# A fused decoder layer on one core: two more pairs by seven products in the down projection, and the low parts of 14 tiles made by an accumulating DMA

## The chip, the core and the metric

The kernel runs on one core of a Trainium2 chip. The metric is the device time of one execution in microseconds (us), the median of several runs: 1047.4 us for the kernel before (three runs, 1047.33 to 1047.88).

## The reference

One layer with 256 tokens and width 2048: two kinds of attention side by side, an output projection, and an MLP. Only the MLP's second product matters here, `u @ w_down`, where `u` is 256 x 8192 and `w_down` 8192 x 2048, all float32:

```python
x = x + _rmsnorm(mixed @ w_out[layer], norm_attn_post[layer])

h = _rmsnorm(x, norm_mlp_pre[layer])
u = jnp.square(jax.nn.relu(h @ w_up[layer]))
x = x + _rmsnorm(u @ w_down[layer], norm_mlp_post[layer])
```

## The kernel before, in words

**Three passes for one float32 product.** TensorE multiplies in the rounded type fp32r. So each operand is split into a high part `hi` (the value rounded, written by ScalarE, ACT, L306) and a low part `lo` (the value less its high part, a subtraction on VectorE, DVE, L307). A product is `hi*hi + hi*lo + lo*hi`, three matmuls of 128x128 by 128x512 (`three`, L1016).

**The down projection** (from L1197) has two halves `c`, each 1024 columns of `w_down`. In a half the 64 row blocks of 128 rows, `k`, go by in order; two of them make a pair `kp`. There are two ways through a pair:

- *ordinary* (`"k"`): each of the two row blocks is a tile of 128x1024 (512 KB), loaded by SP into one of five buffers `raw`, split by ACT and DVE into `hi` and `lo` (eight buffers each), and used by 4 products: 8 products, 24 matmuls in the pair.
- *by seven products* (`"w"`): the pair is treated as a 2x2 block matrix by a Strassen-like scheme (`seven_products`, L1021): 7 products, 21 matmuls, but from four tiles (`b11`, `b`, `u`, `t`). The pair's 1,024 KB come by one DMA on GpSimd's queue (POOL, L374) into the buffers `ab_down` and `c` in turn (`load_two`, `seven_down`). DVE forms sums of them (`sums`, L361, L365, L366) into `st_down`, and the four tiles are split as ordinary tiles are. The left operand needs sums too: three small DVE instructions (`four_sums`, L977 to L979, into `st_down`) and a split into `s`.

`DOWN_SEVEN` (L117) lists the pairs by seven products: 7, 11, 13, 17, 19, 23, 25 and 29 in the first half, the odd ones from 3 to 27 in the second. `SHARED` lists those in both; their `s` is written to DRAM in the first half (`keep_s`) and read back in the second (`down_back`, POOL). In the first half the low parts `ulo` of `u`, one group for every two pairs, are made on DVE and written to DRAM (`keep_u`); the second half reads them back on POOL (L960).

**What sets the order.** Everything is written out at build time; each engine and each DMA queue works through its own list in order, and semaphores hold an instruction until its operands and its buffer are ready. `Weights.emit` (L193) writes a tile's load and split seven tiles ahead of its products. `plan_seven` (L406) hangs a seven-product pair's `fetch` and `sums` in front of the tile that is two tiles before the pair's first (`SUMS_AHEAD`), though not before the end of the preceding seven-product pair. Where seven-product and ordinary pairs alternate, `fetch` and `sums` of a pair therefore stand right behind the four tiles of the seven-product pair before it, and in front of the ordinary pair in between. `Weights.emit` is where ordinary tiles are split.

Of the kernel before, what the change touches and what calls it, by code (L numbers as in the profile page):

```python
# [18 lines left out]
F32 = mybir.dt.float32  # L19
# [3 lines left out]
AF = mybir.ActivationFunctionType  # L23
OP = mybir.AluOpType
# [77 lines left out]
def up_steps(first, *groups):  # L102
    steps = [("k", k) for k in first]
    for i, ks in enumerate(groups):
# [9 lines left out]
N_SEVEN = [sum(w == "w" for w, _ in steps) for steps in UP_STEPS]  # L114


DOWN_SEVEN = ((7, 11, 13, 17, 19, 23, 25, 29), range(3, 28, 2))  # L117
SHARED = [k for k in DOWN_SEVEN[0] if k in DOWN_SEVEN[1]]
GT = FF // 512
DOWN_STEPS = [[s for kp in range(2 * GT)  # L120
               for s in ([("w", kp)] if kp in ws else [("k", 2 * kp), ("k", 2 * kp + 1)])] for ws in DOWN_SEVEN]

# [5 lines left out]
class Flow:  # L128
# [3 lines left out]
    def __init__(self):  # L132
        self.clock = 0.0
        self.chains = []
# [34 lines left out]
class Weights:  # L169


    def __init__(self, nc, pool, split, bufs, ahead):
        self.nc, self.pool, self.split_fn = nc, pool, split
        self.bufs, self.limit, self.ahead = bufs, bufs, ahead
        self.specs, self.tiles, self.done = [], [], []
        self.first, self.after = {}, {}

    def plan(self, *spec):


        self.specs.append(spec)
        self.done.append(False)
        return len(self.specs) - 1
# [9 lines left out]
    def emit(self, upto):  # L193
        upto = min(upto, self.done.index(False) + self.limit, len(self.specs))
        while len(self.tiles) < upto:
            i = len(self.tiles)
            spec = self.specs[i]
            make = len(spec) == 1
            for f in self.first.pop(i, ()):
                f()  # L200
            if not make:
                src, nk, n, g = (*spec, None)[:4]
                w = nk * n
                raw = self.load(src if len(src.shape) == 3 else src.rearrange("(k p) n -> p k n", p=P), w, f"raw{i}")
                for f in self.after.pop(i, ()):
                    f()
            hi = self.pool.tile([P, CW], F32R, tag="hi", bufs=self.bufs, name=f"hi{i}")
            lo = self.pool.tile([P, CW], F32R, tag="lo", bufs=self.bufs, name=f"lo{i}")
            if make:
                spec[0](hi, lo)  # L210
                self.tiles.append((hi, lo))
                continue

            def v(t):
                return t[:, :w].rearrange("p (k n) -> p k n", k=nk)

            cuts = [(o, min(o + 512, w)) for o in range(0, w, 512)] if i < FINE else [(0, w)]
            for o, e in cuts:
                self.split_fn(hi[:, o:e], lo[:, o:e], raw[:, o:e], g)
            self.tiles.append((v(hi), v(lo)))  # L220
# [43 lines left out]
def layer(nc, tc, io):  # L264
# [52 lines left out]
    weights = Weights(nc, wp, split, W_BUFS, W_AHEAD)  # L317
# [23 lines left out]
    def up_weight(j, k):  # L341
        return io["w_up"][k * P:(k + 1) * P, j * CW:(j + 1) * CW]
# [34 lines left out]
    def seven_up(j, kp):  # L377
        def load():
            if UP_PAIRS[j][kp] == "raw":
                return [weights.load(up_weight(j, 2 * kp + i), CW, f"raw_w{j}_{kp}{i}") for i in range(2)]  # L380
            return load_two(late[UP_PAIRS[j][kp]], nc.gpsimd if (j, kp) > (1, 0) else nc.sync,
                            io["w_up"][2 * kp * P:(2 * kp + 2) * P, j * CW:(j + 1) * CW])

        return seven(load, lambda: [late["up"].tile([P, CW], F32, tag="T", bufs=2, name=f"{n}{j}_{kp}") for n in "tu"])
# [21 lines left out]
    def plan_seven(fetch_sums, fs, after, more=(), late_sums=0, last=()):  # L406

        at = max(len(weights.specs) - SUMS_AHEAD, after)
        fetch, sums = fetch_sums
        for n, f in (*more, (0, fetch), (-late_sums, sums), *((0, f) for f in last)):  # L410
            weights.first.setdefault(at - n, []).append(f)
        return [weights.plan(f) for f in fs], len(weights.specs)
# [4 lines left out]
    for j in range(FF // CW):  # L417
        wide_u.append([])
        for what, k in UP_STEPS[j]:
            if what == "k":  # L420

                ts = [weights.plan(up_weight(j, k), 1, CW, *([gcol[:, 8 + k:9 + k]] if j < 2 or k >= 2 * max(N_SEVEN) else []))]
            else:
                ts, after = plan_seven(*seven_up(j, k), after, (), SUMS_AHEAD + 1 if not k and N_SEVEN[j - 1] else 0)
            wide_u[j].append((what, k, ts))

    def down_weight(c, k):
        return io["w_down"][k * P:(k + 1) * P, c * CW:(c + 1) * CW]

    def seven_down(c, kp):  # L430
        def load():

            n = DOWN_SEVEN[c].index(kp)
            raw = dpl["ab"]
            if n % 2:
                raw = late["u01" if c else "c"]
            return load_two(raw, nc.gpsimd, io["w_down"][2 * kp * P:(2 * kp + 2) * P, c * CW:(c + 1) * CW])

        return seven(load, lambda: [late["st"][:, i * CW:(i + 1) * CW] for i in range(2)])

    dpl, left, skeep, wide_d = {}, {}, {}, []
    for c in range(2):
        wide_d.append([])
        for what, k in DOWN_STEPS[c]:
            if what == "k":
                ts = [weights.plan(down_weight(c, k), 1, CW)]
            else:
                q, parts_q, back = [lambda c=c, k=k, f=f: f(c, k) for f in (down_sums, down_split, down_back)]
                more = {"last": (back,)} if c and k in SHARED else {"more": ((2, q), (1, parts_q))}
                ts, after = plan_seven(*seven_down(c, k), after, **more)  # L450
            wide_d[c].append((what, k, ts))
# [451 lines left out]
    for ns in ((0, 1), (2,), (3,)):  # L903
# [4 lines left out]
        for c, b, acc in proj(mixT, [ch_o[n] for n in ns], f"o{ns[0]}", order, heads_done):  # L908
            n = ns[c]
            if not late:  # L910
# [8 lines left out]
                                  in_=io["norm_attn_post"].partition_broadcast(P).rearrange("p o d -> p (o d)"))  # L919
# [131 lines left out]
    for j in range(FF // CW):  # L1051
# [9 lines left out]
        for t, b in order:  # L1061
            what, k, tiles = steps[t]
# [18 lines left out]
            if what == "k":  # L1081
                w = weights.get(tiles[0])
                h_done(k, b)
                for n in range(2):
                    c = slice(n * 512, (n + 1) * 512)
# [111 lines left out]
    for c in range(2):  # L1197
# [3 lines left out]
        accs = {(b, n): y[b][2 * c + n] for b, n in PARTS}  # L1201
        ws = DOWN_SEVEN[c]
        for t, (what, k, tiles) in enumerate(wide_d[c]):
# [4 lines left out]
            if what == "k":  # L1208
                w = weights.get(tiles[0])
# [37 lines left out]
    for g in (GT - 2, GT - 1):  # L1247
        for b, n in PARTS:
            for kk in range(4):
                k = 4 * g + kk  # L1250
                w = weights.get(tail[k])
# [39 lines left out]
def build(nc, arrays):  # L1291
    io = {n: nc.dram_tensor(f"in_{n}", a.shape, mybir.dt.from_np(a.dtype), kind="ExternalInput").ap()
          for n, a in arrays.items()}
    io["out"] = nc.dram_tensor("out_0", (S, D), F32, kind="ExternalOutput").ap()
    with tile.TileContext(nc) as tc, tc.manual_schedule():
        layer(nc, tc, io)
# [12 lines left out]
```

## Time and profile before

| | |
|---|---|
| median of three runs | 1047.4 us |
| profiled execution, first to last instruction (span) | 1045.7 us |
| median less span | 1.7 us |
| down projection, first `y` matmul to last | 701.6 to 1037.1 us |
| matmuls of 128x512 in the first half | 744 (24 pairs x 24 + 8 pairs x 21) |

The profiled execution has a span and no total of its own; what lies around the span is taken as the 1.7 us between it and the median. Times in a row are us from the span's start unless marked ns. A matmul's row lasts 0.39 us, but matmuls overlap: the pace, start to start, is what counts. Rows `A <- B` in a list of waits say how long the first stood idle and what ended it; in such rows `SPq` is SP's DMA queue. Line numbers with rows of the profile are those of the kernel before; in lists of the changed kernel a line is 9 to 11 higher.

### The profile page before, as it was taken

The page shows a single profiled execution, that of the slowest core. Times are in us where ns is not written, and L with a number is a line of the kernel's source. Part 1 is how long each engine was busy: PE and PEld are TensorE (multiplying, and loading weights), DVE is VectorE, ACT ScalarE, POOL GpSimd, SP SyncE. Part 2 cuts the span into 40 slices and gives each one's busy share as a digit, 9 for nine tenths or more (in the row PEclk, how much of TensorE's full clock was granted, in tenths as well). Part 3 has the DMA queues.
Part 4 walks back from the last instruction along what each step waited for, and adds up shares of the span by engine and source line. Part 5 has one row for each costly group of instructions (what it writes and reads, how often), then busy time and mean ns, then how long its engine had stood idle before and what let it go on. Part 6 is the DMA issues. An engine that isn't in the chain of part 4 may idle for free.

```text
span 1045.7 us, 13378 instructions
## 1 busy us (share of the span) xinstructions
PE 1035.7 (99%) x4837; PEld 863.2 (83%) x4837; DVE 838.7 (80%) x1122; ACT 630.4 (60%) x848; POOL 51.5 (5%) x83
## 2 busy tenths in 40 slices
PE   9999999999999999999999999999999999999996
PEld 6888889888888888888888888888888888888885
DVE  6676536567557669999999999897899978999995
ACT  6674436565545566665765667666567564766661
POOL 0000000000000000000000000000000000111100
PEclk9999999999999999999999999999999999999998
DMA  9975547454447295646657356378778767698952
GB/s 303 370 229 148 140 129 241 146 162 153 150 156 236 92 360 188 216 147 207 202 185 246 121 201 207 113 253 325 274 276 303 265 232 261 238 332 323 356 204 83
DMA packets 79938, 229.33 MB, mean 219 GB/s; under 512 B 6912, under 2 KB 11520, under 8 KB 79488
## 3 DMA queue, kind: packets, MB, share of 16 engines
q1 hardware_dynamic: 64576, 171.47, 48.9%
q0 software_dynamic: 14864, 56.63, 15.2%
q8 instruction: 38, 0.62, 0.3%
q10 hardware_dynamic: 432, 0.37, 0.1%
q14 instruction: 28, 0.23, 0.1%
HBM read 212.72 MB, written 15.73 MB: 218 GB/s over the span
## 4 chain that ended last, share of the span: by engine, by line
PE 97%; DVE 1%; issue 1%; ACT 0%; POOL 0%; DVEq 0%; POOLq 0%; ACTq 0%
PE y L296 25%; PE acc_u L296 24%; PE acc_o L296 8%; PE m L296 7%; PE md L296 5%; PE acc_qk L296 4%; PE acc_v L296 4%; PE acc_ckv L296 2%; PE acc_ukv L296 2%; PE acc_q L296 2%; PE acc_cq L296 2%; PE acc_k L296 2%; PE acc_uq L296 2%; PE rt L300 1%; PE sc_b L296 1%
## 5 line engine op out<-in xcount | busy, mean ns | idle before, releaser
L307 DVE TENSOR_TENSOR lo<-raw,hi 128x1024 fp32r<-128x1024 f32 (+3 forms) x213 | 241.5, 1152 | 89.8 <-ACT hi L306 89.1
L306 ACT ACTIVATE hi<-raw 128x1024 fp32r<-128x1024 f32 (+3 forms) x213 | 209.9, 999 | 73.6 <-PE y L296 16.1
L296 PE MATMUL y<-hi,uhi 128*128 128x512 f32 x370 | 144.4, 390 | 0.0
L296 PE MATMUL y<-hi,ulo 128*128 128x512 f32 x370 | 144.1, 389 | 0.0
L296 PE MATMUL y<-lo,uhi 128*128 128x512 f32 x370 | 144.0, 389 | 0.0
L296 PE MATMUL acc_u<-hi,hT_hi 128*128 128x512 f32 x356 | 141.7, 398 | 0.0
L296 PE MATMUL acc_u<-hi,hT_lo 128*128 128x512 f32 x356 | 139.2, 391 | 0.4 <-DVE hT_lo L307 0.4
L296 PE MATMUL acc_u<-lo,hT_hi 128*128 128x512 f32 x356 | 138.9, 390 | 0.0
L311 DVE SCALAR_TENSOR_TENSOR lo<-raw,gcol,hi 128x1024 fp32r<-128x1024 f32 x74 | 92.5, 1279 | 9.5 <-ACT hi L310 9.5
L310 ACT ACTIVATE hi<-raw,gcol 128x1024 fp32r<-128x1024 f32 x74 | 83.7, 1148 | 25.0 <-DMA raw<-in_w_up 11.7
L296 PEld LDWEIGHTS y<-hi,ulo 128*128 128x128 f32 x370 | 69.5, 188 | 14.4
L296 PEld LDWEIGHTS y<-lo,uhi 128*128 128x128 f32 x370 | 69.5, 188 | 14.3
L296 PEld LDWEIGHTS y<-hi,uhi 128*128 128x128 f32 x370 | 69.5, 188 | 14.2
L296 PEld LDWEIGHTS acc_u<-hi,hT_lo 128*128 128x128 f32 x356 | 66.8, 188 | 14.9 <-DVE hT_lo L307 0.8
L296 PEld LDWEIGHTS acc_u<-lo,hT_hi 128*128 128x128 f32 x356 | 67.0, 188 | 12.8
L296 PEld LDWEIGHTS acc_u<-hi,hT_hi 128*128 128x128 f32 x356 | 67.0, 188 | 12.8
L306 ACT ACTIVATE hi<-u 128x1024 fp32r<-128x1024 f32 (+1 forms) x38 | 37.4, 990 | 49.2 <-DVE u L366 35.4
L307 DVE TENSOR_TENSOR lo<-st_down,hi 128x1024 fp32r<-128x1024 f32 x42 | 50.4, 1220 | 3.0 <-ACT hi L306 2.8
L296 PE MATMUL acc_o<-hi,mixT_hi 128*128 128x512 f32 x128 | 51.8, 405 | 0.0
L306 ACT ACTIVATE hi<-st_down 128x1024 fp32r<-128x1024 f32 x42 | 43.9, 1052 | 12.6 <-PE y L296 9.5
L296 PE MATMUL acc_o<-hi,mixT_lo 128*128 128x512 f32 x128 | 50.2, 392 | 0.0
L296 PE MATMUL acc_o<-lo,mixT_hi 128*128 128x512 f32 x128 | 50.0, 391 | 0.0
(328 smaller groups left out, 2087.7 us busy)
## 6 DMA issues: line engine op xcount, KB each, us to landing
raw<-in_w_down SPq DMA_DIRECT2D x86, 512.0 KB, 5.8
raw<-in_w_up SPq DMA_DIRECT2D x76, 512.0 KB, 4.6
raw<-in_w_in SPq DMA_DIRECT2D x55, 512.0 KB, 4.9
ab<-in_w_up POOLq DMA_DIRECT2D x22, 1024.0 KB, 5.4
raw<-in_w_out SPq DMA_DIRECT2D x32, 512.0 KB, 4.2
ab_down<-in_w_down POOLq DMA_DIRECT2D x11, 1024.0 KB, 7.1
ukeep<-ulo SPq DMA_DIRECT2D x15, 512.0 KB, 7.0
ulo<-ukeep POOLq DMA_DIRECT2D x15, 512.0 KB, 6.2
```

Source lines behind the costliest of these rows:

```text
L296: nc.tensor.matmul(out, a, b, start=start, stop=stop)
L300: nc.tensor.transpose(out, a, ident)
L306: nc.scalar.activation(hi, src, AF.Copy)
L307: nc.vector.tensor_tensor(out=lo, in0=src, in1=hi.bitcast(F32), op=OP.subtract)
L310: nc.scalar.activation(hi, src, AF.Copy, scale=g)
L311: nc.vector.scalar_tensor_tensor(out=lo, in0=src, scalar=g, in1=hi.bitcast(F32), op0=OP.mult, op1=OP.subtract)
```

## The change

```diff
-DOWN_SEVEN = ((7, 11, 13, 17, 19, 23, 25, 29), range(3, 28, 2))
+DOWN_SEVEN = ((7, 10, 13, 15, 17, 19, 21, 23, 25, 29), range(3, 28, 2))
+LO_BY_DMA = [(0, 2 * kp) for kp in (6, 8, 9, 11, 12, 14, 16, 18, 20, 22, 24, 26, 27, 28)]
...
         self.first, self.after = {}, {}
+        self.lo_by_dma = set()
...
+            if i in self.lo_by_dma:
+                self.nc.scalar.activation(hi[:, :w], raw[:, :w], AF.Copy)
+                self.nc.scalar.activation(lo[:, :w], hi[:, :w].bitcast(F32), AF.Copy, scale=-1.0)
+                self.nc.gpsimd.dma_start(out=lo[:, :w].bitcast(F32), in_=raw[:, :w], accum_op=OP.add)
+                self.tiles.append((v(hi), v(lo)))
+                continue
...
                 ts = [weights.plan(down_weight(c, k), 1, CW)]
+                if (c, k) in LO_BY_DMA:
+                    weights.lo_by_dma.add(ts[0])
```

In the first half, pairs 10, 15 and 21 go by seven products and pair 11 no longer does. From pair 13 to pair 25 every second pair is now of that kind. From pair 6 to pair 28, the first of the two tiles of each ordinary pair gets its low part in another way: ACT writes `-hi` into `lo`, and a DMA from SBUF to SBUF on POOL's queue adds `raw` to it. `SHARED` grows from seven pairs to eight (15 and 21 join, 11 leaves).

POOL's list, from the first half's fetch of pair 19 on, before (`c` and `ab_down` are fetches of pairs by seven products; `ulo` is the first row of the second half):

```order
L374 DMA ab_down<-in_w_down 128x2x1024
L374 DMA c<-in_w_down 128x2x1024
L374 DMA ab_down<-in_w_down 128x2x1024
L374 DMA c<-in_w_down 128x2x1024
L374 DMA ab_down<-in_w_down 128x2x1024
L960 DMA ulo_1_7701<-ukeep_6483 128x1024
```

and after the change, from the fetch of pair 15 to that of pair 21 (L222 is the accumulating DMA, of the first tile of pairs 14, 16 and 18):

```order
L383 DMA c<-in_w_down 128x2x1024
L222 DMA lo_6817<-raw_6814 128x1024
L383 DMA ab_down<-in_w_down 128x2x1024
L222 DMA lo_6909<-raw_6906 128x1024
L383 DMA c<-in_w_down 128x2x1024
L222 DMA lo_7001<-raw_6998 128x1024
L383 DMA ab_down<-in_w_down 128x2x1024
```

What moved: before, one fetch stands right behind the other; now an accumulating DMA, which waits for ACT, stands ahead of each fetch.

ACT's list before, from the high part of pair 19's `s` to the two tiles of pair 20 (`uhi` is the high part of a group of `u`):

```order
L306 ACTIVATE s_19_6957<-st_down 128x512
L306 ACTIVATE hi_6960<-st_down 128x1024
L306 ACTIVATE hi_6982<-raw_6980 128x1024
L306 ACTIVATE uhi_9_7000<-uT_5213 128x1024
L306 ACTIVATE hi_7006<-raw_7004 128x1024
```

and the like place after, from pair 17's `s` to the two tiles of pair 16, where `lo_6909` is the negated high part:

```order
L315 ACTIVATE s_17_6887<-st_down 128x512
L315 ACTIVATE hi_6890<-st_down 128x1024
L220 ACTIVATE hi_6908<-raw_6906 128x1024
L221 ACTIVATE lo_6909<-hi_6908 128x1024
L315 ACTIVATE uhi_8_6927<-uT_5193 128x1024
L315 ACTIVATE hi_6933<-raw_6931 128x1024
```

What moved: one more instruction stands behind the first `hi<-raw`, and POOL's `lo_6909` waits for it. Behind `s_17` on ACT stands everything that leads to that DMA.

DVE's list after the change, from the sums of pair 17 (fetched into `ab_down`) to the left operand's sums of pair 19 (L988 to L990):

```order
L370 TENSOR_TENSOR st_down<-ab_down 128x1024
L374 TENSOR_TENSOR st_down<-st_down,ab_down 128x512
L375 TENSOR_TENSOR st_down<-st_down,ab_down 128x512
L316 TENSOR_TENSOR ulo_8_6928<-uT_5193,uhi_8_6927 128x1024
L316 TENSOR_TENSOR lo_6934<-raw_6931,hi_6933 128x1024
L316 TENSOR_TENSOR lo_6950<-ab_down,hi_6949 128x512
L316 TENSOR_TENSOR lo_6957<-ab_down,hi_6956 128x1024
L988 TENSOR_TENSOR st_down<-uT_5213 128x256
L989 TENSOR_TENSOR st_down<-st_down,uT_5213 128x128
L990 TENSOR_TENSOR st_down<-uT_5213,st_down 128x128
```

What moved: one `lo<-raw` stands between the sums and `b11`'s low part, where two stood before.

## The prediction

> **What bounds the kernel now.** I read the page first (span, busy shares, the chain that ended last), then a table by stretches of 20 us for the first half of the down projection, then that chain in order of time.
>
> ```profile
> span 1045.7 us, 13378 instructions
> ...
> PE 1035.7 (99%) x4837; PEld 863.2 (83%) x4837; DVE 838.7 (80%) x1122; ACT 630.4 (60%) x848; POOL 51.5 (5%) x83
> ...
> PE 97%; DVE 1%; issue 1%; ACT 0%; POOL 0%; DVEq 0%; POOLq 0%; ACTq 0%
> ```
>
> ```profile
> 740.00:760.00 20.00, 20.00 (x90) 16.58 (x89) 19.16 (x24) 12.04 (x14) 0.71 (x1) 1.00 0.83 304
> 760.00:780.00 20.00, 20.00 (x90) 16.57 (x89) 17.84 (x20) 13.96 (x15) 0.71 (x1) 1.00 0.80 278
> 780.00:800.00 20.00, 20.00 (x90) 16.56 (x89) 18.29 (x22) 11.87 (x13) 1.43 (x2) 1.00 0.78 266
> 800.00:820.00 20.00, 20.00 (x90) 16.55 (x89) 19.16 (x24) 11.81 (x14) 0.71 (x1) 1.00 0.92 343
> 820.00:840.00 20.00, 20.00 (x90) 16.57 (x89) 17.72 (x21) 14.14 (x16) 0.71 (x1) 1.00 0.77 268
> 840.00:860.00 20.00, 20.00 (x90) 16.57 (x89) 15.10 (x14) 11.13 (x12) 0.00 (x0) 1.00 0.58 199
> ```
>
> ```profile
> 746.46 16.32 PE y L296 x72
> ```
>
> The columns of the table are: stretch, its length, busy time of PE, weight load, DVE, ACT and POOL, granted clock, share of the DMA engines, GB/s. TensorE is the bound and has no gap: 20.00 of 20, clock 1.00. So a matmul fewer is time won, and any wait that reaches it is time lost. One matmul is 16.32 / 72 = 0.227 us. DVE is nearly as full (15.1 to 19.2 of 20), the DMA engines 0.58 to 0.92, ACT 11 to 14. TensorE does not wait because the splits run ahead until the eight `hi` buffers are full, which is what ended most of ACT's idle time here:
>
> ```profile
> ACT hi L306 <- PE y L296: 32.3, 30, 2.1
> ```
>
> **What it takes off.** Two more pairs by seven products: 2 x 3 matmuls x 0.227 = **1.36 us** off TensorE, 0.13% of the time. That is all that can be won, since nothing else is on the path.
>
> **DVE and ACT.** One period of an ordinary and a seven-product pair in the trace of before, on DVE, from pair 23's sums to pair 25's:
>
> ```profile
> 806.59 1.22 DVE L361 TENSOR_TENSOR st_down<-c 128x1024 f32<-128x1024 f32 x1
> 807.84 0.69 DVE L365 TENSOR_TENSOR st_down<-st_down,c 128x512 f32<-128x512 f32 x1
> 808.57 0.69 DVE L366 TENSOR_TENSOR st_down<-st_down,c 128x512 f32<-128x512 f32 x1
> 809.17 2.35 DVE L307 TENSOR_TENSOR lo<-raw,hi 128x1024 fp32r<-128x1024 f32 x2
> 811.45 0.68 DVE L307 TENSOR_TENSOR lo<-c,hi 128x512 fp32r<-128x512 f32 x1
> 812.05 1.22 DVE L307 TENSOR_TENSOR ulo<-ab,uhi 128x1024 fp32r<-128x1024 f32 x1
> 813.18 1.22 DVE L307 TENSOR_TENSOR lo<-c,hi 128x1024 fp32r<-128x1024 f32 x1
> 814.32 0.42 DVE L977 TENSOR_TENSOR st_down<-ab 128x256 f32<-128x256 f32 x1
> 814.77 0.29 DVE L978 TENSOR_TENSOR st_down<-st_down,ab 128x128 f32<-128x128 f32 x1
> 815.10 0.29 DVE L979 TENSOR_TENSOR st_down<-ab,st_down 128x128 f32<-128x128 f32 x1
> ...
> 816.44 0.69 DVE L307 TENSOR_TENSOR s<-st_down,s 128x512 fp32r<-128x512 f32 x1
> ...
> 818.30 1.22 DVE L361 TENSOR_TENSOR st_down<-ab_down 128x1024 f32<-128x1024 f32 x1
> ```
>
> ```profile
> L306 ACT ACTIVATE hi<-raw 128x1024 fp32r<-128x1024 f32 x34 | 35.5, 1057 | 12.0 <-PE y L296 11.1 <-ACT hi L306 0.8
> ...
> L306 ACT ACTIVATE s<-st_down 128x512 fp32r<-128x512 f32 x7 | 4.4, 633 | 10.0 <-DVE st_down L979 10.0
> ```
>
> By these rows a seven-product pair costs DVE 2.60 (sums) + 1.00 (three small ones) + 0.69 (`s`) + 0.68 + 3 x 1.22 (four low parts) = 8.6 us, an ordinary pair 2 x 1.22 = 2.4. Two more pairs add 12.4 us; 14 low parts fewer take 14 x 1.22 = 17.1 away: 4.7 us less in all. ACT gets 14 x 1.06 = 14.8 us of negations and about 2 x 2.3 for the two pairs, 19 us over some 169 us: its 11 to 14 of 20 become 13 to 16, so its work hides; its place in a chain doesn't (below). In the second half the eighth shared pair takes 1.7 us from DVE and moves 2 x 512 KB by DMA; TensorE is full there too and nothing is gained.
>
> In the stretch that now alternates (pairs 13 to 25, six periods) a period takes DVE 818.30 - 806.59 = 11.71 us, no gap in it, less the 1.13 from start to start of one `lo<-raw`: 10.58. TensorE needs 45 x 0.227 = 10.20. So DVE falls behind by 0.4 a period, 2.3 us in all, which the full buffers can cover.
>
> **The added wait.** The accumulating DMA waits on POOL's queue for ACT's negation. Queued behind it is the next pair's fetch, and DVE's sums wait for that. Before, POOL had nothing else in its list, so it fetched as soon as a buffer was free:
>
> ```profile
> 783.42 0.71 POOL L374 DMA_DIRECT2D c<-in_w_down  x1 [17.21 <-DVE lo L307]
> 796.78 0.72 POOL L374 DMA_DIRECT2D ab_down<-in_w_down  x1 [12.64 <-DVE lo L307]
> ```
>
> The fetch at 783.42 was for the sums at 806.59, and the one at 796.78 for those at 818.30: 21 to 23 us ahead, with a landing in 6 to 9. That lead goes. Now the work closes into a ring. From the sums of pair 15 DVE reaches the left operand's sums for pair 17; ACT then does `s`, `hi` of tile `t`, `hi` of pair 16's first tile, its negation; POOL issues the accumulating DMA, then the fetch of pair 19; its landing releases the sums of pair 19, two periods after those of pair 15. The first part: 815.10 + 0.29 - 806.59 = 8.80, less 1.13, is 7.67 us on DVE; 0.63 + 3 x 1.06 = 3.81 on ACT; 0.55 for the DMA's issue (the next fence). Together 12.03. Two periods of TensorE are 20.40. So TensorE loses nothing as long as a fetch lands within **8.4 us** of its issue.
>
> How long it takes, from rows: issues in the first half, then in the second, and the issue of a 512 KB DMA on POOL.
>
> ```profile
> raw<-in_w_down SPq DMA_DIRECT2D x51, 512.0 KB, 5.9
> ...
> ab_down<-in_w_down POOLq DMA_DIRECT2D x5, 1024.0 KB, 6.1
> c<-in_w_down POOLq DMA_DIRECT2D x4, 1024.0 KB, 8.9
> ```
>
> ```profile
> ulo<-ukeep POOLq DMA_DIRECT2D x14, 512.0 KB, 6.3
> u<-in_w_down POOLq DMA_DIRECT2D x6, 1024.0 KB, 8.4
> ab_down<-in_w_down POOLq DMA_DIRECT2D x6, 1024.0 KB, 8.8
> ```
>
> ```profile
> L960 POOL DMA_DIRECT2D ulo<-ukeep x15 | 8.3, 555 | 95.3 <-PE y L296 95.3
> ```
>
> A fetch alone takes (5 x 6.1 + 4 x 8.9) / 9 = 7.3 us. Ahead of it in the same queue is now the accumulating DMA. No row shows one. 512 KB more on POOL cost 8.6 - 6.3 = 2.3 us by the second fence. Lower end: it passes like a plain copy, 2.3, and a fetch takes 9.6. Upper end: 9.2, four times that, as far as I can stretch these rows. I take twice, 4.6, because it has to read `raw` and `lo`, 1,024 KB, to write 512, which is nearest to the 1,024 KB rows. Then a fetch takes 11.9, the ring 12.03 + 11.9 = 23.9, and TensorE loses 3.5 us in two periods, three times between pair 13 and pair 25: **10.6 us**.
>
> The Trainium skill's page "Collectives: The Full Stack", section "The bandwidth ceiling: the fold count and why AG ≠ RS ≠ AR", says that the DMA engines' add itself is free, but that it needs two source reads per write, so that such a transfer runs at half a copy's rate. No run here shows it yet; by it the sum is the one I took, and by its other half alone (the add is free, so a copy's price) the sum would be that of the second rival.
>
> Two smaller terms. The full buffers cover part of the loss: eight tiles are some 12.6 us of products here, of which a pair's sums and splits need about half, so 0 to 6. Pair 29 has its fetch behind the accumulating DMA of pair 27, with only three tiles between that tile and its own four, 4 x 12 x 0.227 = 10.9 us of products against 0.55 + 11.9 + 2.60 + one `hi` and one `lo` (2.3) = 17.4, less a lead of perhaps 5: 0 to 4. I let these two cancel, and keep their ends.
>
> `raw` is held until the accumulation lands. One cycle of a buffer is then 5.9 (load) + 1.06 + 1.06 + 0.55 + 8.6 = 17 us plus waiting, while five buffers at two tiles per 10.2 us allow 25: covered.
>
> **Sum:** 10.6 - 1.36 = +9.2, ends +3 and +13. On the span, 1045.7 + 9.2 = 1054.9; with the 1.7 us around it (median 1047.4) **1056.6 us**.
>
> **Rivals.**
> *Hidden after all.* The accumulation passes beside the fetch rather than ahead of it, and a fetch lands within 8.4 us. TensorE keeps its 1.36 us, DVE's 2.3 us are covered or not: 1046.0 to 1048.4 us, not slower. For it: 6.1 us for `ab_down`, and buffers that are full when the stretch begins; at a copy's price the ring loses 12.03 + 9.6 - 20.4 = 1.2 us in two periods, 3.7 in all, and the buffers can cover that. It decides at 8.4 us. Against it:
>
> ```profile
> DMA packets 13271, 48.42 MB, mean 277 GB/s; under 512 B 1346, under 2 KB 1346, under 8 KB 13260
> ```
>
> In the 175 us around the first half 48.4 MB moved; 14 x 1.05 MB more, with both reads counted, make 63.1, or 361 GB/s, where 343 GB/s already meant a share of 0.92. The engines would be full on average.
>
> *Slow accumulation.* At four times a copy's price a fetch takes 7.3 + 9.2 = 16.5 us, the ring loses 8.1 in two periods, 24.4 in all, pair 29 some 4 more: 24.4 + 4 - 1.4 = +27, 1074 us. For it: the engines would be over full, and a negated tile's own `lo` may come late too. Against it: nothing in the trace.
>
> *The change doesn't do what it says:* the program does hold six matmuls fewer and 14 such DMAs, so this has no chance to speak of.
>
> **Numbers.** Differences under 0.2% (2.1 us) can hardly be told from no change. The forecast (1050 to 1066) 0.45; hidden 0.26; slow accumulation (over 1066) 0.24; the rest, 0.05, holds a gain over 0.2% by something that I don't see, 0.03. So faster 0.03, the same 0.26, slower 0.71. The range takes in the hidden case whole and reaches up to the slow one: 1046 to 1075. Forecast and slow case lie on one side and hold 0.69; the forecast's own range is 1050 to 1066.
>
> **What would show it.** Right: from about pair 15 on, stretches of the first half with TensorE under 20 of 20; DVE's sums of `c` and `ab_down` wait for their DMA; POOL's fetch issues about 11 us before the sums that use it, not 21 to 23; fetches landing in about 12 us; the second half unchanged. Hidden: fetches land under 8.4 us and TensorE stays full. Slow: accumulating DMAs that land in over 15 us, and TensorE waiting for a `lo` that a DMA writes. Wrong altogether if the time appears in the second half, or if TensorE's pace itself changes from 0.227 us.

## The result, and the profile after

The changed kernel takes **1066.6 us** (median of four runs, 1062.91 to 1067.38) against 1047.45 us for the kernel before on the same chip (four runs, 1047.33 to 1047.88): 19.2 us more by the medians. The ratio of the means is 1.0175, with a 95% interval of 1.0161 to 1.0188. The profiled execution took 1066.72 us with a span of 1064.9, 19.2 us over the span of before. Line numbers in rows of the changed kernel are 9 to 11 above those of before; they shift by a few more in the experiments.

The page of the changed kernel, its span, its busy times and the chain of work that ended last:

```profile
span 1064.9 us, 13402 instructions
...
PE 1041.9 (98%) x4831; PEld 863.6 (81%) x4831; DVE 832.5 (78%) x1122; ACT 645.0 (61%) x867; POOL 65.5 (6%) x100
...
PE 89%; DMA 4%; issue 3%; DVE 2%; ACT 1%; POOL 0%; SPq 0%; POOLq 0%; DVEq 0%; ACTq 0%
```

TensorE's share of the chain fell from 97% to 89%, and DMA, which was not among the entries shown before, holds 4%. TensorE has six matmuls fewer (x4831 for x4837), as the change says, yet 6 us more of busy time, so some matmuls were slower too. The table by stretches of 20 us says where (stretch, its length, busy time of PE, weight load, DVE, ACT, POOL, granted clock, share of the DMA engines, GB/s):

```profile
740.00:760.00 20.00, 20.00 (x90) 16.58 (x89) 12.29 (x15) 12.70 (x14) 2.45 (x3) 1.00 0.87 252
760.00:780.00 20.00, 16.31 (x63) 12.49 (x62) 13.80 (x17) 10.87 (x14) 3.20 (x4) 0.91 1.00 326
780.00:800.00 20.00, 19.30 (x84) 15.34 (x83) 17.54 (x23) 12.53 (x15) 1.60 (x2) 1.00 1.00 315
800.00:820.00 20.00, 17.11 (x74) 13.55 (x73) 17.89 (x24) 13.19 (x15) 3.19 (x4) 1.00 1.02 326
820.00:840.00 20.00, 19.51 (x86) 15.79 (x85) 18.09 (x22) 15.44 (x18) 2.45 (x3) 1.00 0.95 305
840.00:860.00 20.00, 19.70 (x86) 15.68 (x85) 9.58 (x12) 12.00 (x13) 4.04 (x5) 1.00 0.90 277
860.00:880.00 20.00, 15.76 (x58) 11.93 (x57) 16.65 (x16) 11.99 (x13) 0.00 (x0) 0.83 0.84 271
```

The number behind PE's busy time is the handiest measure in this document: an undisturbed stretch counts 90 matmuls (89 now and then), at 0.227 us each. Missing here are 27 from 760 to 780, 6 + 16 + 4 + 4 = 30 from 780 to 860, and 32 from 860 to 880: 89 matmuls, 20.2 us. Less the 1.36 us that six matmuls fewer save, that makes 18.8 of the 19.2 us. Before 740 and behind 880 us TensorE is as full as it was. So the time went in three places: the fetch of the seven-product pair 13 (6.1 us), the stretch from pair 15 to pair 25 in which every second pair goes by seven products (6.8 us; "the ring" below), and the fetch of pair 29 (7.3 us). "At pair 13" and "at pair 29" below name the pair whose fetch came late; TensorE itself stops one pair earlier, as the rows will show.

What TensorE waited for, over the whole kernel (the kernel before has no such row in this stage):

```profile
PE y L305 <- DMA lo<-raw: 6.0, 7, 2.5
PE y L305 <- DVE ulo L316: 4.0, 2, 3.1
PE y L305 <- ACT uhi L315: 2.2, 2, 1.6
```

What DVE waited for, 700 to 895 us:

```profile
DVE st_down L370 <- DMA c<-in_w_down: 20.1, 4, 12.2
DVE st_down L370 <- DMA ab_down<-in_w_down: 10.4, 3, 6.6
```

And how long DMAs took from issue to landing there (the last two rows are the fetches, 7.3 us on average before):

```profile
lo<-raw POOLq DMA_DIRECT2D x14, 512.0 KB, 7.6
ab_down<-in_w_down POOLq DMA_DIRECT2D x6, 1024.0 KB, 10.8
c<-in_w_down POOLq DMA_DIRECT2D x5, 1024.0 KB, 12.0
```

DVE now stands 30 us before its sums because fetches come late. Three waits make up most of it: 5.9 us at pair 10, which cost TensorE nothing, 6.6 at pair 13 and 12.2 at pair 29; those in the ring are 0.3 to 2.2 us. Counted to the moment when DVE was free for the sums, the fetches of pairs 17 to 25 had a lead of 9 to 11 us, those of pairs 10, 13 and 29 only 3.5, 4.2 and 2.4. Pair 29 on POOL, on DVE, on ACT and on TensorE, in order of time:

```profile
847.71 0.86 POOL L222 DMA_DIRECT2D lo<-raw  x1 [3.09 <-PE md L305]
848.25 1.05 POOL L383 DMA_DIRECT2D c<-in_w_down  x1
851.76 0.86 POOL L222 DMA_DIRECT2D lo<-raw  x1 [2.46 <-PE md L305]
```

```profile
862.88 1.23 DVE L370 TENSOR_TENSOR st_down<-c 128x1024 f32<-128x1024 f32 x1 [12.20 <-DMA c<-in_w_down]
...
867.22 1.22 DVE L316 TENSOR_TENSOR ulo<-uT,uhi 128x1024 fp32r<-128x1024 f32 x1
```

```profile
862.94 0.63 ACT L315 ACTIVATE hi<-c 128x512 fp32r<-128x512 f32 x1 [10.38 <-PE y L305]
863.48 1.04 ACT L315 ACTIVATE uhi<-uT 128x1024 fp32r<-128x1024 f32 x1
```

```profile
862.56 0.39 PE L305 MATMUL y<-hi,ulo 128*128 128x512 f32 x1
864.57 0.50 PE L305 MATMUL y<-hi,uhi 128*128 128x512 f32 x1 [1.62 <-ACT uhi L315]
866.76 0.80 PE L305 MATMUL y<-lo,uhi 128*128 128x512 f32 x1 [1.68 <-DMA lo<-raw]
868.49 0.80 PE L305 MATMUL y<-hi,ulo 128*128 128x512 f32 x1 [0.93 <-DVE ulo L316]
869.08 0.63 PE L305 MATMUL y<-hi,uhi 128*128 128x512 f32 x1
869.51 0.63 PE L305 MATMUL y<-lo,uhi 128*128 128x512 f32 x1
```

The fetch stands right behind the accumulation of pair 27 and lands 14.6 us after its issue (848.25 to 862.88). DVE stood idle for 12.2 us and has no time to spare now: first the sums, then two low parts, and only at 867.22 the `ulo` that TensorE needs. ACT, too, comes to `hi<-c` only with the landing, and `uhi` stands behind that. TensorE has not even reached pair 29: it stops at the first tile of pair 28, which shares the group `uhi`, `ulo` with pair 29. It stops three times between 862.56 and 868.49: for `uhi`, for that tile's own `lo`, whose accumulation was issued at 851.76 and took 15.0 us, and for `ulo`. Then it goes on at 0.43 us from matmul to matmul instead of 0.227. Pair 13 is the same case: TensorE stands at the first tile of pair 12, for the `ulo` that is written behind pair 13's sums:

```profile
772.70 0.50 PE L305 MATMUL y<-hi,ulo 128*128 128x512 f32 x1 [3.05 <-DVE ulo L316]
```

### The profile page after: what moved, and what is told of

Read it like the earlier page. It is cut to its first block, busy times and chain, and to the rows that moved or that the text cites. A ratio compares the mean times of both kernels' runs of the same rounds, so it can differ in the third digit from the quotient of the medians.

```text
span 1064.9 us, 13402 instructions
## 1 busy us (share of the span) xinstructions
PE 1041.9 (98%) x4831; PEld 863.6 (81%) x4831; DVE 832.5 (78%) x1122; ACT 645.0 (61%) x867; POOL 65.5 (6%) x100
## 3 DMA queue, kind: packets, MB, share of 16 engines
q0 software_dynamic: 17568, 66.59, 19.2%
## 4 chain that ended last, share of the span: by engine, by line
PE 89%; DMA 4%; issue 3%; DVE 2%; ACT 1%; POOL 0%; SPq 0%; POOLq 0%; DVEq 0%; ACTq 0%
PE acc_u L305 24%; PE y L305 20%; PE acc_o L305 8%; PE m L305 7%; PE md L305 4%; PE acc_v L305 4%; PE acc_qk L305 4%; DMA lo<-raw 3%; PE acc_ckv L305 2%; PE acc_ukv L305 2%; PE acc_q L305 2%; PE acc_cq L305 2%; PE acc_k L305 2%; PE acc_uq L305 2%; PE rt L309 1%
## 5 line engine op out<-in xcount | busy, mean ns | idle before, releaser
L316 DVE TENSOR_TENSOR lo<-raw,hi 128x1024 fp32r<-128x1024 f32 (+3 forms) x195 | 219.9, 1145 | 84.6 <-ACT hi L315 83.8
L315 ACT ACTIVATE hi<-raw 128x1024 fp32r<-128x1024 f32 (+3 forms) x195 | 191.3, 993 | 71.6 <-DMA raw<-in_w_in 17.0
L305 PE MATMUL y<-hi,ulo 128*128 128x512 f32 x358 | 141.3, 395 | 4.0 <-DVE ulo L316 4.0
L305 PE MATMUL y<-hi,uhi 128*128 128x512 f32 x358 | 141.5, 395 | 2.2 <-ACT uhi L315 2.2
L316 DVE TENSOR_TENSOR lo<-st_down,hi 128x1024 fp32r<-128x1024 f32 x46 | 55.3, 1220 | 2.3 <-ACT hi L315 2.3
L315 ACT ACTIVATE hi<-st_down 128x1024 fp32r<-128x1024 f32 x46 | 47.6, 1050 | 9.2 <-DVE st_down L375 6.3
```

The source lines that it names most:

```text
L305: nc.tensor.matmul(out, a, b, start=start, stop=stop)
L315: nc.scalar.activation(hi, src, AF.Copy)
L316: nc.vector.tensor_tensor(out=lo, in0=src, in1=hi.bitcast(F32), op=OP.subtract)
```

## The experiments

Two theories stood after the first look. **Place**: the fetch has to wait behind a DMA that waits for ACT, so its lead of 21 to 23 us shrinks to 11 and less. **Weight**: an accumulating DMA is a heavy transfer, and 14 of them fill the DMA engines (share 0.90 to 1.02 in the ring, 0.58 to 0.92 in the same stretches before). Rivals: ten pairs without a gap between them, whatever the DMAs; and, later, the order of the splits on ACT.

All runs in one table. "More" is the median less that of the kernel before on the same chip; "missing" counts the matmuls that fail to 90 in the stretches of 20 us, as above (at pair 13, in the ring from 780 to 860 us, at pair 29), from one profiled execution of each. The ratio is that of the means. The profiled execution of the copy in place of the add is the slowest of its four, 1061.4 us, so its counts make more than its median.

| run | median us | more | ratio, 95% interval | missing: 13, ring, 29 |
|---|---|---|---|---|
| the change | 1066.6 | 19.2 | 1.0161 to 1.0188 | 27, 30, 32 |
| ten pairs, no DMA | 1051.0 | 3.0 | 1.0019 to 1.0038 | 0, 19, 0 |
| eight pairs, with the DMAs | 1066.2 | 18.2 | 1.0156 to 1.0192 | 26, 31, 22 |
| copy in place of the add | 1059.0 | 11.0 | 1.0095 to 1.0125 | 6, 39, 20 |
| early fetches | 1056.4 | 8.4 | 1.0064 to 1.0094 | 0, 37, 0 |
| early for pairs 10, 13, 29 | 1059.8 | 12.2 | 1.0094 to 1.0128 | 0, 58, 0 |
| late sums for 10, 13, 29 | 1062.8 | 15.2 | 1.0132 to 1.0162 | 6, 37, 23 |
| early fetches, copy | 1051.4 | 3.8 | 1.0022 to 1.0045 | 0, 20, 0 |
| early fetches, late `s` | 1057.2 | 9.6 | 1.0076 to 1.0106 | 0, 50, 0 |
| early, 3 adds | 1053.6 | 6.0 | 1.0040 to 1.0068 | 0, 29, 0 |
| early, 7 adds | 1053.8 | 6.1 | 1.0047 to 1.0072 | 0, 24, 0 |
| early, 3 adds outside the ring | 1051.4 | 3.5 | 1.0021 to 1.0048 | 0, 18, 0 |
| early, 3 adds, late `s` | 1052.0 | 4.2 | 1.0030 to 1.0055 | 0, 17, 0 |

The table leaves out a small loss in the second half. In every experiment with ten pairs TensorE waits there once for the `ulo` that is read back, 0.2 to 0.8 us, and 3 to 5 matmuls are missing from 960 to 1000 us; with early fetches 5 more are missing from 900 to 920 us. The change, which comes to the second half later, has no such wait.

### One half of the change at a time

**Ten pairs, no DMA.** All low parts stay on DVE.

```diff
-LO_BY_DMA = [(0, 2 * kp) for kp in (6, 8, 9, 11, 12, 14, 16, 18, 20, 22, 24, 26, 27, 28)]
+LO_BY_DMA = []
```

> Ten pairs by seven products, all low parts on DVE again; nothing accumulates. Three theories of the loss of 19 us. Place: the fetches stand behind the accumulating DMAs in POOL's list, come late, and DVE idles in front of its sums. Weight: the accumulating DMAs read two operands each and fill the DMA engines. Split: ten pairs are more than DVE can do. Place and weight both expect this kernel to lose only DVE's overload, (11.71 - 10.20) x 6 = 9 us less what the full buffers cover (0 to 9): 1046 to 1055 us. Split expects 1060 us or more, since DVE has even more to do here.

Measured: 3.0 us more. DVE is full in the ring, and TensorE's only new waits in the first half are for it (stretches of the ring, then TensorE's waits):

```profile
800.00:820.00 20.00, 19.43 (x85) 15.44 (x83) 19.66 (x25) 13.40 (x16) 1.43 (x2) 1.00 0.86 275
820.00:840.00 20.00, 18.16 (x76) 14.29 (x77) 19.83 (x23) 11.87 (x14) 1.43 (x2) 1.00 0.68 229
```

```profile
PE y L305 <- DVE ulo L316: 1.7, 3, 0.6
...
PE y L305 <- DVE lo L316: 0.7, 2, 0.4
```

So DVE without relief gives up 4.4 us, more than the 1.36 us that the matmuls save; ten pairs by themselves are a small loss, not the 19 us.

**Eight pairs, with the DMAs.** The old list of pairs, 14 low parts by DMA (pair 11 is by seven products again, so pair 10 takes its place in the list).

```diff
-DOWN_SEVEN = ((7, 10, 13, 15, 17, 19, 21, 23, 25, 29), range(3, 28, 2))
-LO_BY_DMA = [(0, 2 * kp) for kp in (6, 8, 9, 11, 12, 14, 16, 18, 20, 22, 24, 26, 27, 28)]
+DOWN_SEVEN = ((7, 11, 13, 17, 19, 23, 25, 29), range(3, 28, 2))
+LO_BY_DMA = [(0, 2 * kp) for kp in (6, 8, 9, 10, 12, 14, 16, 18, 20, 22, 24, 26, 27, 28)]
```

> The eight pairs of before, and 14 low parts by an accumulating DMA (in the first tile of pairs 6, 8, 9, 10, 12, 14, 16, 18, 20, 22, 24, 26, 27, 28). Place: two or three accumulating DMAs stand ahead of every second fetch, so DVE idles there and TensorE loses nearly as much as in the change: 1057 to 1068 us. Weight: the DMA engines carry the same 14 accumulations: 1060 to 1068 us. Split: no third kind of work, under 1050 us.

Measured: 18.2 us more, with nothing saved to set against it. One row each of TensorE's and of DVE's waits:

```profile
PE y L305 <- DMA lo<-raw: 8.1, 3, 5.0
```

```profile
DVE st_down L370 <- DMA c<-in_w_down: 27.3, 3, 11.6
```

The DMAs alone make nearly the whole loss, in the same two kinds of wait. What the extra pairs do is not the question any more; what the DMAs do is.

### Weight against place

**Copy in place of the add.** Same DMA, same place, same bytes written, no addition.

```diff
-                self.nc.gpsimd.dma_start(out=lo[:, :w].bitcast(F32), in_=raw[:, :w], accum_op=OP.add)
+                self.nc.gpsimd.dma_start(out=lo[:, :w].bitcast(F32), in_=raw[:, :w])
```

> The change with its 14 DMAs in their places, but as plain copies of raw over lo instead of additions: it leaves out the addition, so the output is not the reference's. Place: the order and the waits are the same, so most of the loss stays: a fetch lands 2 us earlier, 4 to 8 us less in all, 1057 to 1063 us. Weight: one read instead of two takes half of the added load away, 1048 to 1054 us. Split: 1066 us as the change.

Measured: 11.0 us more, so the addition is worth about 8 of the 19 us and the rest stays. Landings, 700 to 895 us:

```profile
lo<-raw POOLq DMA_DIRECT2D x14, 512.0 KB, 6.1
ab_down<-in_w_down POOLq DMA_DIRECT2D x6, 1024.0 KB, 9.9
c<-in_w_down POOLq DMA_DIRECT2D x5, 1024.0 KB, 11.3
```

Against the change a copy lands in 6.1 us instead of 7.6, and the fetch behind it gains only 0.7 to 0.9 us.

**Early fetches.** In the first half a fetch is written right behind the tiles of the seven-product pair two before, that is ahead of the accumulating DMA, so that it no longer waits for ACT.

```diff
-    def plan_seven(fetch_sums, fs, after, more=(), late_sums=0, last=()):
+    def plan_seven(fetch_sums, fs, after, more=(), late_sums=0, last=(), early=None):
...
+        if early is not None:
+            weights.first.setdefault(early, []).append(fetch)
+            fetch = lambda: None
...
+                early = None if c or not ends else ends[-2] if len(ends) > 1 else ends[0] - 4
-                ts, after = plan_seven(*seven_down(c, k), after, **more)
+                ts, after = plan_seven(*seven_down(c, k), after, early=early, **more)
+                ends.append(after)
```

> The change with each fetch of the first half written right behind the tiles of the pair two before it (whose buffer it takes), so ahead of the accumulating DMAs that it stood behind. The accumulations stay. Place: DVE no longer waits for its sums; TensorE keeps some of its 1.4 us or loses DVE's 2.3: 1046 to 1050 us. Weight: the same bytes, the same loss, 1060 us or more. Split: 1066 us.

Measured: 8.4 us more, so place is worth some 11 us. DVE has no wait for a fetch left, and pairs 13 and 29 lose nothing. Nearly all that is left stands in the ring, in one kind of wait (TensorE's):

```profile
PE y L305 <- DMA lo<-raw: 6.4, 5, 2.3
```

**Early fetches and copy.** Both edits at once, the place of the fetch as in the run before and this line:

```diff
-                self.nc.gpsimd.dma_start(out=lo[:, :w].bitcast(F32), in_=raw[:, :w], accum_op=OP.add)
+                self.nc.gpsimd.dma_start(out=lo[:, :w].bitcast(F32), in_=raw[:, :w])
```

> Early fetches as in the fourth experiment, and the 14 DMAs as plain copies of raw over lo (it leaves out the addition, so the output is not the reference's). Early fetches with the addition cost 8.4 us. Weight: that rest is the addition's second read, so it goes: 1046 to 1050 us. Chain: the rest is the chain of ACT's negation, POOL and the DMA's landing, which a copy has too, only some 2.5 us shorter in landing: 1051 to 1055 us.

Measured: 3.8 us more. In this arrangement the addition is worth 4.6 us. The two queues and the landing of `lo` from 700 to 895 us, with the addition and then without it (q0 is POOL's queue, q1 SP's; packets, MB, share of 16 engines' time):

```profile
q0 software_dynamic: 5685, 21.45, 40.5%
...
lo<-raw POOLq DMA_DIRECT2D x14, 512.0 KB, 8.9
```

```profile
q0 software_dynamic: 5840, 22.02, 32.9%
...
lo<-raw POOLq DMA_DIRECT2D x14, 512.0 KB, 6.9
```

With fewer bytes counted, the queue's packets take 7.6 points more of 195 us, 14.8 us of all 16 engines over 14 DMAs: 1.06 us each. A copy of 512 KB takes 0.329 x 195 / 22.02 x 0.524 = 1.53 us of them. So an accumulation weighs about 1.7 copies, an estimate that leaves out what the fetches' own packets lose to the crowd. The Trainium skill's page "Collectives: The Full Stack", section "The bandwidth ceiling: the fold count and why AG ≠ RS ≠ AR", says of ReduceScatter that the add needs two source reads per write and so halves the rate; the trace agrees with the direction and nearly with the size, in the time of the packets (1.7). From issue to landing it shows less, 1.2 to 1.3 times a copy (7.6 against 6.1, 8.9 against 6.9).

### The two stops outside the ring

**Early for pairs 10, 13 and 29 alone.** The same edit, only for these pairs:

```diff
+                early = None if c or k not in (10, 13, 29) else ends[-2] if len(ends) > 1 else ends[0] - 4
```

> The change with only the fetches of pairs 10, 13 and 29 written early (behind the tiles of the pair two before); those of the alternating stretch, 15 to 25, stay behind the accumulating DMAs. Short notice: the waits of TensorE at pairs 13 and 29 (about 6 and 7.5 us with the slow clock behind them) come from these fetches, which have one ordinary pair less of notice than the others, and from the left operand's low part ulo that stands behind DVE's sums: those 13 go, 1052 to 1056 us. Ring: the alternating stretch is what delays everything up to pair 29, so most stays: 1060 us or more.

**Late sums.** Fetches stay where the change has them, but DVE comes to the sums of these three pairs two tiles later, so that it doesn't stand before them while other low parts are due.

```diff
-                ts, after = plan_seven(*seven_down(c, k), after, **more)
+                ts, after = plan_seven(*seven_down(c, k), after,
+                                       late_sums=2 if not c and k in (10, 13, 29) else 0, **more)
```

> The change with DVE's sums of pairs 10, 13 and 29 written two tiles later, directly in front of the pair's own tiles, so that the splits of the ordinary tiles and the ulo that stood behind them need not wait; the fetches stay late. Short notice with ulo behind the sums: TensorE's waits for ulo and uhi at pairs 13 and 29 go, it waits for the pair's own b11 instead, some 2 to 4 us less at each: 1058 to 1063 us. If the late fetch alone counts and not what is queued behind it: 1066 us as the change.

Measured: 12.2 and 15.2 us more, so 7.0 and 4.0 us back. Both take the stop at pair 13 away (0 and 6 missing of 27), the early fetch that at pair 29 too. But the ring then loses more: 58 and 37 missing, not 30. The likely reading is that a stop of TensorE lets the splits run ahead, and so pays part of the next loss; no run shows this by itself. The three places don't add up.

The run of all early fetches differs from the one for pairs 10, 13 and 29 only in the fetches of the ring, pairs 15 to 25. So the late fetches of pairs 10, 13 and 29 cost 19.2 less 12.2, 7.0 us, and with these early the late fetches of the ring cost 12.2 less 8.4, 3.8 us. With every fetch early the ring still has 37 matmuls missing, and no wait of DVE for a fetch: that loss has another cause.

### What is left in the ring

**Early fetches, late `s`.** In the ring ACT splits the left operand's sums into `s` ahead of the tile whose low part the DMA makes. Here `s` comes three tiles later.

```diff
-                more = {"last": (back,)} if c and k in SHARED else {"more": ((2, q), (1, parts_q))}
+                more = {"last": (back,)} if c and k in SHARED else {"more": ((2, q), (1 if c else -2, parts_q))}
```

> Early fetches, the additions as in the change, and in the first half the split of the left operand's sums (s on ACT) written three tiles later, behind the high part and the negation of the ordinary tile instead of ahead of them. In the fourth experiment ACT stood 2.7 us in each period in front of s, until TensorE let go of a buffer of it, and the negation behind it came as much later. Chain: the negation and its DMA go 2.7 us earlier, which TensorE lacked by 1.5 to 2 us a period: 1047 to 1051 us. Weight: the same bytes, no change from 1056.

Measured: 9.6 us more against 8.4: no gain, and the theory falls that the order of splits alone holds the loss. The trace shows why, at the longest stop (POOL's issue of the accumulation, then TensorE):

```profile
789.63 0.86 POOL L222 DMA_DIRECT2D lo<-raw  x1 [2.12 <-ACT lo L221]
```

```profile
798.53 0.39 PE L305 MATMUL y<-hi,uhi 128*128 128x512 f32 x1
802.92 0.80 PE L305 MATMUL y<-lo,uhi 128*128 128x512 f32 x1 [4.00 <-DMA lo<-raw]
```

The DMA does start sooner, but 2.9 us behind the fetch of 786.78 in the same queue, and takes 13.2 us to land.

**Three and seven of the 14 adds**, with early fetches.

```diff
-LO_BY_DMA = [(0, 2 * kp) for kp in (6, 8, 9, 11, 12, 14, 16, 18, 20, 22, 24, 26, 27, 28)]
+LO_BY_DMA = [(0, 2 * kp) for kp in (12, 16, 20)]
```

and

```diff
+LO_BY_DMA = [(0, 2 * kp) for kp in (6, 9, 12, 16, 20, 24, 27)]
```

> The change with the fetch of the eighth products written early (as in the run of all early fetches), and only three of the 14 accumulating DMAs (tiles of pairs 12, 16, 20); the other eleven low parts are made by VectorE. Two theories of what is left when the place is mended. (A) Each accumulation takes its share of the DMA engines and nothing else: the loss runs in a straight line from 3.0 us with none (ten pairs, no DMA) to 8.4 us with 14, so with three about +4.2 us, 1051.9 us. (B) Accumulations cost only where they stand close together, and a few of them relieve VectorE, which was full without any (19.7 to 19.9 of 20 us): below the loss with none, +0.5 to +2 us, 1048.3 to 1049.8 us, VectorE under 19.5 of 20 us from 780 to 860 us, TensorE's waits for lo by DMA at most 1 us in all. If it comes out under 1047.0 us, a version beats the kernel before.

> The same with seven of the accumulating DMAs (tiles of pairs 6, 9, 12, 16, 20, 24, 27), so one in every second pair of the stretch. (A) straight line: 3.0 + 7/14 x 5.4 = +5.7 us, 1053.3 us. (B) cost only where they stand close: +1 to +3 us, 1048.8 to 1050.8 us, landing of lo at about 7 us instead of 8.9, TensorE's waits for lo by DMA under 2 us against 6.4.

Measured: 6.0 and 6.1 us more. Seven adds fit the straight line (5.7), and three lie at the edge of what it allows (4.2, with an interval of 4.2 to 7.1); the other theory misses both. The traces show something that neither had: the loss of the first half is **one stop**, at the same accumulation in both runs, that of pair 20. With three adds, ACT, POOL and TensorE there:

```profile
801.30 0.63 ACT L315 ACTIVATE s<-st_down 128x512 fp32r<-128x512 f32 x1 [4.69 <-issue]
...
802.79 1.04 ACT L220 ACTIVATE hi<-raw 128x1024 fp32r<-128x1024 f32 x1
```

```profile
800.53 0.71 POOL L383 DMA_DIRECT2D c<-in_w_down  x1 [11.06 <-DVE lo L316]
805.24 0.92 POOL L222 DMA_DIRECT2D lo<-raw  x1 [3.99 <-ACT lo L221]
```

```profile
809.30 0.39 PE L305 MATMUL y<-hi,uhi 128*128 128x512 f32 x1
813.45 0.79 PE L305 MATMUL y<-lo,uhi 128*128 128x512 f32 x1 [3.76 <-DMA lo<-raw]
```

From the start of `hi` to the landing of `lo` are 813.45 - 802.79 = 10.7 us, where `hi` and a low part on DVE take 2.3. TensorE came to this tile 10.7 - 3.8 = 6.9 us after `hi` began. It stands for 3.76 us, and eleven matmuls after that start 0.43 us apart: another 11 x 0.2 = 2.2 us. With the gaps at its edges that is the 29 missing matmuls, 6.6 us, or 5.2 of the 6.0 after the 1.36 us saved.

**Three adds outside the ring** (pairs 8, 12 and 27), and **three adds with late `s`** (pairs 12, 16 and 20 again), both with early fetches.

```diff
+LO_BY_DMA = [(0, 2 * kp) for kp in (8, 12, 27)]
```

```diff
+LO_BY_DMA = [(0, 2 * kp) for kp in (12, 16, 20)]
...
+                more = {"last": (back,)} if c and k in SHARED else {"more": ((2, q), (1 if c else -2, parts_q))}
```

Both expectations speak of pair 16's accumulation; by the order of POOL's issues, at 758, 783 and 805 us, the late one is pair 20's. It changes nothing else in them.

> Early fetches and three accumulations as in the run with three adds, but for the tiles of pairs 8, 12 and 27, which stand outside the stretch from pair 15 to pair 25 where every second pair goes by seven products. There the accumulation of pair 16 alone stopped TensorE for 3.8 us, and twelve matmuls after it ran at about half pace. (A) What costs is the single accumulation that lands late, by its place: none does here, so the loss is that of ten pairs without any DMA, +2 to +3.5 us, 1049.7 to 1051.2 us, no wait of TensorE for lo by DMA over 0.5 us. (B) Three accumulations cost by their weight on the DMA engines wherever they stand: +5 to +6.5 us again, 1052.7 to 1054.2 us.

> Early fetches, accumulations for pairs 12, 16 and 20 as in the run with three adds, and the split of s three tiles later in the first half, so that ScalarE makes the high part of the tile of pair 16 before it waits for the sums, some 3 to 4 us sooner. (A) What costs is that one accumulation's lateness (0.4 us too little lead would stop TensorE as well, and a stop is followed by half pace): with the lead it lands in time, TensorE stands no time for lo in the stretch, VectorE has room, +0 to +2 us, 1047.7 to 1049.7 us. (B) The stretch has no room for the accumulation whatever its start: the landing stretches or another wait takes its place, +4 to +6 us. Under 1047.0 us a version beats the kernel before.

Measured outside the ring: 3.5 us more, TensorE has no wait for `lo` by DMA at all, and its waits are again those of the run without DMAs:

```profile
PE y L305 <- DVE ulo L316: 1.7, 3, 0.6
```

So three accumulations cost nothing by themselves where there is time; DVE is then again the bound in the ring. Measured with late `s`: 4.2 us more, within what was expected of a stretch without room. The accumulation of pair 20 started 5.4 us sooner than with three adds, and landed only 2.4 us sooner:

```profile
798.50 0.72 POOL L383 DMA_DIRECT2D c<-in_w_down  x1 [11.01 <-DVE lo L316]
799.83 0.92 POOL L222 DMA_DIRECT2D lo<-raw  x1 [0.61 <-ACT lo L221]
```

```profile
811.10 0.50 PE L305 MATMUL y<-lo,uhi 128*128 128x512 f32 x1 [2.03 <-DMA lo<-raw]
```

It took 11.2 us from issue to landing where it had taken 8.2, now 1.3 us behind a fetch and not 4.7. On POOL's queue one of the two always stands behind the other. Right behind an add, a fetch of the first half took 9.4 to 14.6 us in the change; an add less than 3 us behind a fetch took 11.2 to 13.2 in the four cases that the two runs with late `s` have of it. The distance alone does not set it: at 3.2 us behind a fetch three adds of the same two runs took 6.6 to 8.6, and in the change the add of pair 28, 3.5 us behind the fetch of pair 29, took 15.0. That the fetch ahead is what stretches the add fits the first four cases, but no run moved the fetch alone, so it is argued, not shown.

No version beats the kernel before. The nearest are ten pairs without DMAs (3.0 us more), three adds outside the ring (3.5) and early fetches with a copy, which leaves the addition out (3.8).

## Why the prediction was right or wrong, point by point

- **The sign and the added wait: right; where it costs, not.** Slower by the added wait on POOL's queue, in the first half only, DVE's sums waiting for `c` and `ab_down`, fetches that land in 10.8 and 12.0 us (forecast 11.9): the profile after shows each. Early fetches, which take that wait away, bring 11 of 19 us back, but 7.0 of them at pairs 10, 13 and 29 and only 3.8 in the ring, to which the working gave the whole loss.
- **Six matmuls fewer, 1.36 us: right.** 4831 for 4837, the pace of an undisturbed stretch is unchanged, and the second half is as before.
- **DVE and ACT: right.** ACT has 11 to 15 of 20 us, and DVE 17.5 to 18.1 in the ring up to 840. That DVE's relief was needed is shown by the run without DMAs, 19.7 to 19.9 of 20 and 3.0 us more.
- **The price of an accumulation, twice a copy: near.** 1.7 copies by the time of its packets, and fetches in 10.8 and 12.0 us where 11.9 was forecast. That the 11.9 came out is in part luck: behind a copy the fetches still took 9.9 and 11.3, where the working had 9.6, so the second read is worth 0.7 to 0.9 us of their landing and not 2.3. A copy in its place still cost 11.0 us, where the working had let the ring lose 3.7 at a copy's price and called that perhaps hidden. (That price is the first rival's, *Hidden*; the prediction calls it the second's.)
- **The ring, 10.6 us: the place is right, the wait for the most part another.** The stretch lost 6.8 us in the change, so the size is near, but by luck: TensorE stood there for `lo` by DMA and not for the pair's sums. The late fetch, from which the 10.6 were worked out, is worth 3.8 us there (58 matmuls missing with the ring's fetches late and pair 13's stop gone, 37 with all fetches early). The working followed the negation to POOL's queue and to the fetch, but gave no price to the accumulated tile's own `lo`, which it named only in the slow rival: it landed 10.7 us after `hi` began in the run with three adds, where TensorE comes after 6.9.
- **"Two smaller terms … I let these two cancel": this is the step that failed.** Pair 29 was priced at 0 to 4 and lost 7.3 us; pair 13, whose fetch stands behind the accumulation of pair 11 in the same way, had no term at all and lost 6.1. Together 13.4 us against a net of nothing; with the ring 3.8 us below its price, that is 9.6 of the 10.0 us by which the sum fell short. Four things were left out. The working asked when TensorE comes to pair 29's own tiles; it stopped at pair 28's first tile, two tiles sooner, because DVE and ACT, standing before what the fetch brings, hold up the `ulo` and `uhi` behind it (with late sums 4.0 us come back). The lead of the fetch was 2.4 us at pair 29 and 4.2 at pair 13, where the working had perhaps 5. The fetch of pair 29 stands behind two accumulations close together and takes 14.6 us, not 11.9 (pair 13's took 10.8). And the matmuls after a stop are slow, which costs 1.6 to 2.2 us each time.
- **`raw` held until the accumulation lands: covered, as forecast.** SP's queue does wait for it (the row below, 740 to 880 us), but ACT has no wait for a load of `raw` there in the change. With early fetches ACT does wait for loads of `raw`, 7.3 us in five times from 740 to 880 us, so the cover is thin; none of them lies between 775 and 842 us, where TensorE stops in that run.

```profile
SPq L192 <- DMA lo<-raw: 66.5, 12, 12.7
```

- **The rivals.** *Hidden* fails: fetches land above 8.4 us. *Slow accumulation* fails in its price (7.6 us in the median, not over 15, though pair 28's took 15.0), but the sign it named, TensorE waiting for a `lo` that a DMA writes, came true at the lower price.

What stays open: how the loss with early fetches (8.4 us) divides between the longer way of `lo` and the crowd on the DMA engines, since less of the one always changed the other.

## What to carry to other kernels

A DMA that waits for a computation holds up everything behind it on its queue: before putting one there, look for what used to be issued far ahead and check each place where that lead is lost, the single ones at the start and end as much as the regular ones. An engine's work handed to a DMA is late by its landing: here the low part's way grew from 2.3 to 10.7 us, and the tile needs that much more lead, which none of the changes of place tried here gave it in the ring. Don't let two terms cancel that sit at different places; and price a stop at its length plus the slow matmuls that may follow it, 1.6 to 2.2 us here.

## What the runs showed of the hardware

- After some stops TensorE is slow for a while, at 0.43 us from start to start where 0.227 is its pace: eight matmuls after the 3.05 us stop at pair 13, eleven after 3.76 us, eight at pair 29, where three stops of 1.62, 1.68 and 0.93 us lay within 6 us. The granted clock of these stretches is 0.83 to 0.91, against 1.00. The page "TensorE: Matmul & The Clock Gate" of the Trainium skill, Part 1, "The HAM clock gate (the "warmup" mystery)", puts the half rate behind an idle window of about 3.4 us; the trace agrees on the half rate, and shows it also after single stops of 1.91 us (late sums) and 2.03 us (three adds, late `s`), though not after one of 2.54 us in the ring of the change, where the clock stayed at 1.00. So the length of a stop doesn't decide it alone in these runs.
- The issue of a DMA that adds takes POOL 0.86 us in the change, that of a copy in its place 0.55, and it lands 1.2 to 1.3 times as late (7.6 us against 6.1, 8.9 against 6.9).
